# Five stages for split weights, raw transposes in the head, a halved first expert, and w2 stored by output halves

## The chip, the cores and the metric

One NeuronCore of a Trainium2 chip runs the whole kernel. The metric is device time in microseconds of that core: lower is better. A profile of one execution gives the span from its first to its last instruction and what each engine and each DMA queue did in it: PE (matrix products, with PEld for the loading of the stationary operand), DVE (vector), ACT (scalar), POOL, and SP, which here only issues DMAs.

## The reference, cut to what matters

One layer over 256 latent tokens with a context prefix of 256 tokens, D = 1024, all in float32.

```python
mod = silu(c) @ ada_w + ada_b                       # sh1, sc1, g1, sh2, sc2, g2; the same for c_ctx
u  = modulate(rmsnorm(x,   norm1_g), sh1,  sc1)     # modulate(u, shift, scale) = u * (1 + scale) + shift
uc = modulate(rmsnorm(ctx, norm1_g), sh1c, sc1c)
y  = token_mixer(u, uc, ...)                        # u @ w_in, mLSTM (4 heads), differential attention
                                                    # (8 heads), w_branch_a, w_branch_b, gates, w_out
x  = x + g1 * y
x  = x + g2 * moe_ffn(modulate(rmsnorm(x, norm2_g), sh2, sc2))
return rmsnorm(x, final_norm_g)

# moe_ffn: the 4 best of 32 experts for each token; an expert is
hcat  = xf[tok] @ w1[e] + b1[e]                     # w1[e]: 1024 x 2048
h_glu = min(hcat[:, :D_FF], 7);  h_lin = clip(hcat[:, D_FF:], -7, 7)
act   = h_glu * sigmoid(1.702 * h_glu) * (h_lin + 1)
out   = act @ w2[e] + b2[e]                         # w2[e]: 1024 x 1024
```

## The kernel before, in words

The order of the work is written out by hand: each engine takes its instructions in the order in which the program emits them, and semaphores between engines follow from who reads and writes which tile. A tile of a pool with a fixed number of buffers can be written again only when everything that reads its predecessor is done.

**Head.** x and ctx are loaded (L205, L207), their squares summed (L234, L236), and 1/rms made with nine small DVE operations and four diagonal blocks `dg` (L240). `xpose(k)` (L281) multiplies a block of x or ctx by `dg`, which turns and scales it in one product. `ada_first(j)` (L262) makes the shift and scale of 256 channels out of two 1 MB pieces of `ada_w1`, ACT copies the sum (L265), PE turns it (L266) and DVE makes A1 and B1 (L270 to L272). `u_first` (L287 on DVE, L290 on ACT) applies them, `u_second` splits the result in `uh` (ACT cast, L293) and `ul` (DVE, L294). Four rounds j = 0..3 of two channel blocks each are interleaved with the first steps of the first projection chunk.

**Projections.** A `Chunk` is 512 columns of a weight matrix in eight steps of 128 rows. `split(k)` turns raw weights into a rounded part `wh` (ACT, L567) and a remainder `wl` (DVE, L568), in the pool `stg` with 3 buffers of each; `step(k)` multiplies (three products for each result block: L581 to L583 or L591 to L593). A full chunk has 12 products of 512 columns in a step, a half chunk the same count of 256 columns, or six of 512. The main loop emits `split` for up to LOOK = 2 steps ahead, then `step`, then a few ticks of side work: the second part of the modulation (`ada_rest`, L309 and L311, which reads `ada_w2`), the gates, the mLSTM units (L395 to L441), the attention units (L483 to L515) and what follows the chunks. Raw weights, `ada_w1` and `ada_w2` go through a ring of R1 = 4 pieces of 1 MB; a piece is loaded by SP (L159) when its slot is free. At the end come w_branch_b (its evacuation L765, then `late_b`: L771 on DVE, L772 on ACT, L773 on DVE), and w_out, whose second half is first scaled on DVE (`scaled_columns`, L842).

**Experts.** The pools of the projections are closed and their memory becomes places for expert weights (`PLACES`, `ORDER`, `AGAIN`; `slot`, `epiece`, L1014 and L1018): four 2 MB pieces of w1 and two of w2 per expert, 12.6 MB, 32 experts. SP issues a piece when its place is free. `hidden` multiplies (L1070), applies the activation (L1081 to L1085), turns the result (L1090, copied by ACT at L1091); `expert` multiplies with w2 (L1104); `scatter` adds to the sums `xs` (L1125, L1118). Experts 30 and 31 are taken together at the end: `out_half(dh, fh)` loads 512 of the 1024 columns of half a w2 (L1256) and multiplies (L1259), `half_gated` (L1263) and `half_back` (L1269) follow, then the last norm (L1217 to L1225) and the output (L1229 to L1233).

Of the kernel before, what the change touches and what calls it, by code (L numbers as in the profile page):

```python
# [10 lines left out]
F32 = mybir.dt.float32  # L11
# [18 lines left out]
R1, LOOK, LATE = 4, 2, 6  # L30
# [3 lines left out]
HOMES = dict(xc=[0], wk=[1, 2], mk=[3], mv=[4, 5], sums=[6, 7], hm=[8], dk=[1, 3], dv=[2, 4], og=[0], ah=[6], al=[7],  # L34
# [76 lines left out]
def hybrid_layer(ctx: ExitStack, tc, a, out, dbg=None):  # L111
# [40 lines left out]
    fr = ExitStack()  # L152
    ring = fr.enter_context(tc.tile_pool(name="ring", bufs=R1))
# [37 lines left out]
    xs = keep.tile([128, 2, D], F32, name="xs")  # L191
# [38 lines left out]
    xm = [xc[:, 0], xc[:, 1], x1[:, 0], x1[:, 1]]  # L230
    for m in (2, 3, 0, 1):
# [15 lines left out]
    quarters = [(j, h) for j in range(4) for h in range(2)]
    aw = {}

    def ada_load(n):  # L250
        for _ in range(n):
            if quarters:
                j, h = quarters.pop(0)
                aw[j, h] = piece(a["ada_w1"][j, h], 8, 256)

    def ada_first(j):
        q = slice(128 * j, 128 * j + 128)
        for h in range(2):
            for kk in range(4):
                k = 4 * h + kk  # L260
                for g in range(4):
                    mm(S0[32 * g:32 * g + 32, 0, q], sil[:, k, :], aw[j, h][:, 2 * kk + g // 2, 128 * (g % 2):128 * (g % 2) + 128],  # L262
                       start=(k == 0), stop=(k == KT - 1))
        mod = t2([128, 128], "mod0")
        act.copy(mod, S0[:, 0, q])  # L265
        tr(S0[:, 1, q], mod, ident)  # L266
        pv = S0[:, 1, q].rearrange("p (g b s) -> p s g b", g=2, b=2)
        c = slice(2 * j, 2 * j + 2)
        over = lambda v: v[:, None, c].to_broadcast([128, 2, 2])
        dve.tensor_tensor(out=A1[:, :, c], in0=pv[:, 0:2, 1], in1=over(abT[:, 1]), op=OP.add)  # L270
        dve.tensor_tensor(out=B1[:, :, c], in0=pv[:, 0:2, 0], in1=over(abT[:, 0]), op=OP.add)
        dve.tensor_tensor(out=A1[:, :, c], in0=A1[:, :, c], in1=over(ng1), op=OP.mult)  # L272
# [3 lines left out]
    us, xt = {}, {}  # L276

    def xpose(k):
        xt[k] = pp()
        for m in range(4):  # L280
            mm(xt[k][:, m * 128:(m + 1) * 128], xm[m][:, k * 128:(k + 1) * 128], dg[m], start=True, stop=True)  # L281

    def u_first(k):
        us[k] = t2([128, 512], "u")
        for m, s in ((0, slice(256, 512)), (1, slice(0, 256))):
# [1104 lines left out]
```

## Time and profile before

| | us |
|---|---|
| median of 3 runs (lowest, highest) | 1423.0 (1422.38, 1424.02) |
| the profiled execution's own time | 1420.2 |
| its span, first to last instruction | 1418.5 |
| PE busy / DVE busy / ACT busy | 1331.5 / 556.2 / 288.5 |
| DMA read from HBM | 480 MB, 339 GB/s over the span |

The span has three parts: head and projections up to about 488 us, 30 experts in pairs up to about 1310 us, the last two experts and the norm. Busy shares over the whole span say little, since each part has another limit; the rows further down are from views that keep the parts asunder: the span in slices, the chain of waits in order of time, busy time by stretch, single instructions in order of time, and who waited for whom.

### The profile page before, as it was taken

The numbers are of one execution on the slowest core, as the hardware profiler recorded it, in microseconds if no ns is written. First come the engines' busy times: TensorE is split into PE (matmuls) and PEld (weight loads), VectorE is DVE, ScalarE is ACT, GpSimd is POOL, SyncE is SP. The second block draws the span as 40 slices with busy tenths as digits, with TensorE's granted clock in tenths as the row PEclk, the third lists the DMA queues.
The fourth block names the chain that finished last, engine by engine and source line by source line (L and its number), as shares of the span: only waits on it lengthen the run. The fifth ranks groups of instructions, "written<-read, shape, count | busy, mean of one in ns | idle before, by whom it ended". The sixth has DMA issues, their size and how long they took to land.

```text
span 1418.5 us, 17043 instructions
## 1 busy us (share of the span) xinstructions
PE 1331.5 (94%) x6981; PEld 713.5 (50%) x6981; DVE 556.2 (39%) x1181; ACT 288.5 (20%) x620; POOL 36.2 (3%) x55
## 2 busy tenths in 40 slices
PE   5999999999998999999999999999999999999996
PEld 4778777778988734434434433333332333323332
DVE  3586765686667612222222323222212322123113
ACT  3434334444553311101101101011000100001001
POOL 0030001000010000000000000000000000000000
PEclk9999999999999999999999999999999999999999
DMA  9666343223358799999999999999999999999995
GB/s 361 216 250 231 120 156 119 90 90 113 126 190 360 315 369 410 432 429 430 432 428 431 432 429 431 430 430 432 430 431 431 430 429 433 429 430 432 429 416 198
DMA packets 45070, 482.30 MB, mean 340 GB/s; under 512 B 5619, under 2 KB 5876, under 8 KB 11580
## 3 DMA queue, kind: packets, MB, share of 16 engines
q1 hardware_dynamic: 44268, 479.82, 81.9%
q8 instruction: 57, 0.93, 0.2%
q0 software_dynamic: 432, 0.81, 0.2%
q10 hardware_dynamic: 288, 0.52, 0.1%
q14 instruction: 25, 0.20, 0.0%
HBM read 480.08 MB, written 1.06 MB: 339 GB/s over the span
## 4 chain that ended last, share of the span: by engine, by line
PE 58%; DMA 31%; DVE 6%; ACT 2%; issue 1%; SPq 1%; ACTq 0%; DVEq 0%
PE acc L1070 15%; PE py L1104 9%; PE acc L591 4%; PE acc L593 4%; PE acc L592 3%; PE pga L1036 3%; PE acc L581 3%; PE acc L582 3%; DMA v__6686<-in_w_dram 3%; PE acc L583 3%; DMA v__7709<-in_w_dram 3%; DMA v__7935<-in_w_dram 3%; DMA vA__8179<-in_w_dram 3%; DMA v__6212<-in_w_dram 3%; DMA vA__7138<-in_w_dram 3%; DMA v__7364<-in_w_dram 3%
## 5 line engine op out<-in xcount | busy, mean ns | idle before, releaser
L1081 DVE TENSOR_SCALAR eg<-acc 128x512 f32<-128x512 f32 (+1 forms) x33 | 22.3, 675 | 417.1 <-PE acc L1070 417.1
L1082 ACT ACTIVATE es<-eg 128x512 f32<-128x512 f32 (+1 forms) x33 | 20.4, 617 | 687.8 <-DVE eg L1081 687.8
L568 DVE TENSOR_TENSOR wl<-w,wh 128x512 fp32r<-128x512 f32 (+1 forms) x160 | 106.8, 674 | 85.0 <-ACT wh L567 84.2
L1112 DVE TENSOR_TENSOR Y<-py,g2r 64x512 f32<-64x512 f32 x60 | 41.3, 689 | 239.4 <-PE py L1104 238.7
L591 PE MATMUL acc<-uh,wh 128*128 128x256 f32 (+1 forms) x328 | 109.0, 332 | 0.7 <-ACT wh L567 0.7
L567 ACT CAST wh<-w 128x512 fp32r<-128x512 f32 (+1 forms) x160 | 93.1, 603 | 60.9 <-PE acc L583 28.5
L593 PE MATMUL acc<-uh,wl 128*128 128x256 f32 (+1 forms) x328 | 104.3, 318 | 0.3 <-DVE wl L568 0.2
L592 PE MATMUL acc<-ul,wh 128*128 128x256 f32 (+1 forms) x328 | 104.1, 317 | 0.0
L591 PEld LDWEIGHTS acc<-uh,wh 128*128 128x128 f32 x328 | 61.9, 189 | 12.9 <-ACT wh L567 3.9
L581 PE MATMUL acc<-wh,uh 128*128 128x512 f32 x160 | 65.9, 412 | 0.7 <-DVE gi L348 0.7
L593 PEld LDWEIGHTS acc<-uh,wl 128*128 128x128 f32 x328 | 61.7, 188 | 5.6 <-DVE wl L568 0.7
L592 PEld LDWEIGHTS acc<-ul,wh 128*128 128x128 f32 x328 | 61.9, 189 | 4.4 <-DVE ul L294 0.3
L582 PE MATMUL acc<-wl,uh 128*128 128x512 f32 x160 | 63.6, 398 | 0.0
L583 PE MATMUL acc<-wh,ul 128*128 128x512 f32 x160 | 63.5, 397 | 0.0
L815 PE MATMUL acc<-b1s,cst 128*64 128x512 f32 x256 | 61.7, 604 | 0.0
L1036 PE MATMUL pga<-P,x 128*128 128x128 f32 x512 | 60.1, 275 | 0.4 <-DVE P L938 0.4
L1036 PEld LDWEIGHTS pga<-P,x 128*128 128x128 f32 x512 | 58.5, 192 | 0.6 <-DVE P L938 0.5
L1125 PE MATMUL acc<-Y,PGT 128*128 128x512 f32 x120 | 55.8, 606 | 0.0
L311 DVE SCALAR_TENSOR_TENSOR sums<-w,sil,sums 128x512 f32<-128x512 f32 x56 | 42.5, 774 | 0.0
L1118 DVE TENSOR_TENSOR xs<-xs,acc 128x512 f32<-128x512 f32 x60 | 37.4, 679 | 7.0 <-PE acc L1269 7.0
L1070 PE MATMUL acc<-ws,XG 128*64 128x512 f32 x176 | 39.7, 593 | 0.0
L1125 PEld LDWEIGHTS acc<-Y,PGT 128*128 128x128 f32 x120 | 21.5, 189 | 34.0 <-issue 20.8
(680 smaller groups left out, 2088.2 us busy)
## 6 DMA issues: line engine op xcount, KB each, us to landing
ws<-in_w_dram SPq DMA_DIRECT2D x20, 2048.0 KB, 35.2
w<-in_w_in_dram SPq DMA_DIRECT2D x30, 1024.0 KB, 4.8
w<-in_ada_w_dram SPq DMA_DIRECT2D x24, 1024.0 KB, 5.9
w<-in_w_a_dram SPq DMA_DIRECT2D x4, 1024.0 KB, 4.9
wo<-in_w_o_dram SPq DMA_DIRECT2D x4, 1024.0 KB, 4.9
w<-in_w_b_dram SPq DMA_DIRECT2D x4, 1024.0 KB, 9.2
ws<-in_w_dram SPq DMA_DIRECT2D x3, 1024.0 KB, 13.4
wk<-in_w_in_dram SPq DMA_DIRECT2D x2, 1024.0 KB, 13.4
```

The lines of the kernel that those rows point to most:

```text
L567: act.copy(wh[:, 0:n], raw)
L568: dve.tensor_tensor(out=wl[:, 0:n], in0=raw, in1=lanes(wh[:, 0:n]), op=OP.subtract)
L581: mm(self.ps[j], vh[:, k, s], wh, start=st, stop=False)
L582: mm(self.ps[j], vh[:, k, s], wl, start=False, stop=False)
L583: mm(self.ps[j], vl[:, k, s], wh, start=False, stop=sp)
L591: mm(o, wh[:, c], vh[:, k, t0:t1], start=f, stop=False, skip_group_check=g)
L592: mm(o, wh[:, c], vl[:, k, t0:t1], start=False, stop=False, skip_group_check=g)
L593: mm(o, wl[:, c], vh[:, k, t0:t1], start=False, stop=sp, skip_group_check=g)
L1036: mm(p[:, kk, 0:n * CAP], x1[:, tt, k * 128:k * 128 + 128], P[:, tt].rearrange("p e s -> p (e s)"), start=(tt == 0), stop=(tt == 1))
L1070: mm(G[f // 2][64 * (f % 2):64 * (f % 2) + 64], XG[:, k, sw * CAP:sw * CAP + CAP], w[:, f * 512:f * 512 + 512], start=False, stop=(k == KT ...
L1104: mm(Y[r:r + 64], aT_[:, j, fh * 64:fh * 64 + 64], w[:, dh * 512:dh * 512 + 512], start=(kf == 0), stop=(kf == KT - 1))
L1125: mm(p, PGT[parts[dh], 2 * dh + tt, :], Y2[parts[dh], dh], start=True, stop=True)
```

## The change

1. **Stages.** LOOK goes from 2 to 4. A second pool `stg2` with 2 buffers of `wh` and `wl` is added; of five splits in a row three go to `stg`, two to `stg2`. `stg2` takes 8 KB of each partition; the sums `xs` (8 KB) leave the pool `keep` and get a pool of their own after the projections' pools are closed, where `stg2` lay.
2. **Head.** x and ctx are turned raw, before 1/rms is known (`turn`, plain transposes), and copied to two tiles `raw` in the buffers that `mv` uses later. 1/rms is spread over rows by four products (`scale_rows`). `u_of` multiplies raw by it, then applies A1 and B1 for one block. `ada_w1` is stored so that one 1 MB piece serves one block of 128 channels; `ada_first(j)` is for one block, and one product with `fold` (64 columns) adds and turns it. The pieces are loaded in another order: the first ahead of the first projection weights, three more before the second half of these, four as slots come free.
3. **First expert.** Its activation goes in two halves of 256 columns (`parts=2`); the turned gates of the first pair use PSUM bank `py`, not `ptr`; a Sigmoid of one element is issued before the expert loop.
4. **w2.** It is stored with the 512 columns of an output half together. In an expert, both output halves read from the two halves of a piece; in `out_half` a load has 8 KB (the last ones 4 KB) in a row for each partition, where it had rows of 2 KB.
5. **End.** `half_gated` and `half_back` of the last quarter go in two parts of 256 columns; the first output DMA goes through SP, not ACT.

```diff
-R1, LOOK, LATE = 4, 2, 6
+R1, LOOK, LATE = 4, 4, 6
+HOMES: raw=[4, 5]                                  # mv=[4, 5] as before
+    stg2 = fr.enter_context(tc.tile_pool(name="stg2", bufs=2))
-    xs = keep.tile([128, 2, D], F32, name="xs")
+    xs = tp("xs", 1).tile([128, 2, D], F32, name="xs")      # after fr.close()
...
+    def ada_load():
+        if eighths:
+            j = eighths.pop(0)
+            aw[j] = piece(a["ada_w1"][j], 8, 256)
     load_small("ng1T", "ada_bT")
+    ada_load()
...
+    def turn(m):
+        for hf in range(2):
+            p = acc()
+            for k in range(4):
+                tr(p[:, k * 128:k * 128 + 128], xm[m][:, (4 * hf + k) * 128:(4 * hf + k) * 128 + 128], ident)
+            dst, src = raw[hf][:, :, m * 128:m * 128 + 128], p.rearrange("p (k t) -> p k t", k=4)
+            (dve.tensor_copy if hf else act.copy)(dst, src)
     for m in (2, 3, 0, 1):                         # squares as before
+            if m == 3:
+                turn(2)
+                turn(3)
     rs1 = rstd_of(...); dg = ...                   # as before
+    turn(0)
+    turn(1)
...
     def ada_first(j):
+        q = slice(128 * (j % 4), 128 * (j % 4) + 128)
+        for k in range(KT):
+            for b in range(2):
+                g = 2 * (k % 2) + b
+                mm(S0[32 * g:32 * g + 32, 0, q], sil[:, k, :], aw[j][:, k, 128 * b:128 * b + 128],
+                   start=(k < 2), stop=(k >= KT - 2))
+        mods[j] = t2([128, 128], "mod0")
+        act.copy(mods[j], S0[:, 0, q])
+    def ada_turn(j):
+        pt = pp()
+        mm(pt[:, 0:64], mods.pop(j), fold, start=True, stop=True)
+        dve.tensor_scalar(A1[:, :, j], ...); dve.tensor_scalar(B1[:, :, j], ...)
+    def scale_rows():
+        for m in range(4):
+            mm(rsr[0][:, m * 128:m * 128 + 128], ones, dg[m], start=True, stop=True)
+    def u_of(k):
+        dve.tensor_tensor(out=u, in0=raw[k // 4][:, k % 4], in1=rsr[0], op=OP.mult)
+        # then A1, B1 in two halves (k even: DVE, odd: ACT), act.copy to uh, dve subtract to ul
...
     def split(self, k):
-            wh = stg.tile([128, 512], F32R, name="wh")
-            wl = stg.tile([128, 512], F32R, name="wl")
+            at = stg if nsplit[0] % 5 < 3 else stg2
+            nsplit[0] += 1
+            wh = at.tile([128, 512], F32R, name="wh")
+            wl = at.tile([128, 512], F32R, name="wl")
...
     first.load(0)
+    for _ in range(3):
+        ada_load()
     first.load(1)
+    ada_first(0)
+    scale_rows()
+    ada_turn(0)
+    first.split(0)
+    ada_first(1)
+    u_of(0)
+    first.split(1)
+    ada_load()
+    ada_turn(1)
+    for k in range(KT):
+        if k + 2 < KT:
+            ada_first(k + 2)
+        if k + 1 < KT:
+            u_of(k + 1)
+        ada_load()
+        if k + 2 < KT:
+            first.split(k + 2)
+            first.step(k)
+            ada_turn(k + 2)
...
-                mm(Y[r:r + 64], aT_[:, j, fh * 64:fh * 64 + 64], w[:, dh * 512:dh * 512 + 512],
+                mm(Y[r:r + 64], aT_[:, j, fh * 64:fh * 64 + 64], w[dh][:, j * 512:j * 512 + 512],
+    warm = mt.tile([1, 1], F32, name="warm")
+    act.activation(warm, ones[0:1, 0:1], AF.Sigmoid)
-                        nxt["PGT0"] = transposed(PG, 2)
+                        nxt["PGT0"] = transposed(PG, 2, "py")
-            Y = expert(..., gates_turned if (pr, sw) == (LATE, 1) else None)
+            Y = expert(..., gates_turned if (pr, sw) == (LATE, 1) else None, 1 if e else 2)
-            nc.scalar.dma_start(rows_of[:, 0:512], xo[:, tt, 0])
+            (nc.scalar if tt else nc.sync).dma_start(rows_of[:, 0:512], xo[:, tt, 0])
...
     def out_half(dh, fh):
-        step = 2 if dh and fh else 4
-        for k0 in range(0, 4, step):
+        step = 1024 if dh and fh else 2048
+        for k0 in range(0, 2048, step):
             for i in range(2):
-                src = a["w2"][E - 2 + i, fh].rearrange("p (k n) -> p k n", k=4)
-                nc.sync.dma_start(w[i][:, k0:k0 + step], src[:, k0:k0 + step, s])
+                nc.sync.dma_start(w[i][:, k0:k0 + step], a["w2"][E - 2 + i, fh][:, 2048 * dh + k0:2048 * dh + k0 + step])
-    half_gated(1)
-    half_back(1)
+    half_gated(1, 2)
+    half_back(1, 2)
...
-    r["ada_w1"] = f(ada[:, 0:2 * D].reshape(2, 4, 128, 2, 4, 256).transpose(4, 0, 2, 1, 3, 5)).reshape(4, 2, 128, 2048)
+    r["ada_w1"] = f(ada[:, 0:2 * D].reshape(KT, 128, 2, KT, 128).transpose(3, 1, 0, 2, 4)).reshape(KT, 128, 2048)
-    r["w2"] = rows(f(i["exp_w2"]).reshape(E * D, D), 4).reshape(E, 2, 128, 4 * D)
+    r["w2"] = f(f(i["exp_w2"]).reshape(E, 2, 4, 128, 2, 512).transpose(0, 1, 3, 4, 2, 5)).reshape(E, 2, 128, 4 * D)
```

## Rows read from the trace of the kernel before

**Rows 1.** Page, 40 equal slices: DMA rate.

```profile
GB/s 361 216 250 231 120 156 119 90 90 113 126 190 360 315 369 410 432 429 430 432 428 431 432 429 431 430 430 432 430 431 431 430 429 433 429 430 432 429 416 198
```

**Rows 2.** Chain that ended last, in order of time: start us, us, what.

```profile
768.74 33.80 DMA v__5982<-in_w_dram
...
901.65 3.46 PE py L1104 x16
```

**Rows 3.** Busy time of each engine by stretch, PE clock, DMA share, GB/s.

```profile
492.70:510.00 17.30, 16.97 (x94) 8.16 (x96) 4.40 (x24) 2.04 (x6) 0.31 (x1) 1.00 0.94 347
769.00:1330.00 561.00, 526.66 (x2496) 199.40 (x2494) 138.33 (x278) 41.42 (x84) 2.96 (x10) 1.00 1.01 430
1372.00:1400.00 28.00, 25.81 (x111) 8.95 (x108) 5.10 (x11) 1.50 (x4) 0.00 (x0) 1.00 0.94 363
```

**Rows 4.** SP's DMA issues in order of time: start us, us, what.

```profile
520.42 0.33 SPq L1018 DMA_DIRECT2D v__4961<-in_w_dram  x1
...
547.49 0.33 SPq L1018 DMA_DIRECT2D ws<-in_w_dram  x1
```

**Rows 5.** Head, chain in order of time: PE's turning and modulation products.

```profile
13.39 3.74 PE pp L281 x16
...
31.62 1.78 PE pp L281 x16
36.21 1.93 PE S L262 x64
```

**Rows 6.** Head, single instructions: loads that land, and POOL.

```profile
9.67 1.06 ACT L234 ACTIVATE junk<-xc 128x1024 f32<-128x1024 f32 x1 [1.38 <-DMA xc<-in_ctx_dram]
17.07 1.15 ACT L567 CAST wh<-wk 128x512 fp32r<-128x512 f32 x2 [6.24 <-DMA wk<-in_w_in_dram]
43.27 0.77 POOL L146 DMA_DIRECT2D lamr<-in_lam_dram  x1 [0.96 <-PE pp L281]
```

**Rows 7.** First products of the first chunk's steps 6 and 7.

```profile
51.47 0.39 PE L591 MATMUL acc<-uh,wh 128*128 128x512 f32 x1
...
54.34 0.40 PE L591 MATMUL acc<-uh,wh 128*128 128x512 f32 x1
```

**Rows 8.** PE's waits up to 490 us: total us, times, longest us.

```profile
PE pp L429 <- ACT hm L437: 5.4, 4, 2.8
PE acc L591 <- ACT wh L567: 2.2, 3, 0.9
PE acc L581 <- ACT wh L567: 1.7, 1, 1.7
PE acc L593 <- DVE wl L568: 1.4, 4, 0.6
```

**Rows 9.** End of the projections: a single instruction, and the stretch with PE's clock.

```profile
459.45 0.69 DVE L773 TENSOR_TENSOR yl<-tg,yh 128x512 fp32r<-128x512 f32 x1 [0.68 <-ACT yh L772]
455.00:475.00 20.00, 17.93 (x70) 13.27 (x70) 15.43 (x26) 8.73 (x17) 0.00 (x0) 0.91 0.99 407
```

**Rows 10.** First expert, between its two products.

```profile
510.93 1.28 ACT L1082 ACT_TABLE_LOAD   x1 [12.30 <-DVE eg L1081]
513.73 0.63 PE L1090 MATMUL ptr<-cst,el 128*128 128x128 f32 x4 [2.17 <-DVE el L1085]
515.03 5.35 PE L1104 MATMUL py<-v__4796,eaT 128*64 128x512 f32 x16 [0.67 <-ACT eaT L1091]
```

**Rows 11.** Last expert (two halves) and end: waits and issues.

```profile
1382.66 0.42 DVE L1081 TENSOR_SCALAR eg<-acc 128x256 f32<-128x256 f32 x1 [14.37 <-PE acc L1070]
1387.07 0.64 PE L1259 MATMUL pga<-v__8287,eaT 128*64 128x512 f32 x1
1396.07 0.64 PE L1259 MATMUL pga<-ws,v__8216 128*64 128x512 f32 x1 [1.06 <-DMA ws<-in_w_dram]
1412.54 0.72 ACT L1229 ACTIVATE v__8130<-v__8130,rsfy 128x512 f32<-128x512 f32 x1 [0.49 <-ACT v__8130 L1229]
```

**Rows 12.** Page, DMA issues: what, times, KB each, median us to landing.

```profile
w<-in_w_in_dram SPq DMA_DIRECT2D x30, 1024.0 KB, 4.8
```

More of the change, by code (lines that the diff above doesn't have):

```diff
@@ L213, in load_small @@
             nc.sync.dma_start(small[n], a[n])
+    eighths = list(range(KT))
+    aw = {}
+    def ada_load():
+        if eighths:
+            j = eighths.pop(0)
+            aw[j] = piece(a["ada_w1"][j], 8, 256)
     load_small("ng1T", "ada_bT")
+    ada_load()
     sil = sm.tile([128, KT, 32], F32, name="sil")
@@ L230, in hybrid_layer @@
     xm = [xc[:, 0], xc[:, 1], x1[:, 0], x1[:, 1]]
+    raw = [b8([128, 4, 512], "raw") for _ in range(2)]
+    def turn(m):
[5 more added lines that the diff above has]
+            (dve.tensor_copy if hf else act.copy)(dst, src)
     for m in (2, 3, 0, 1):
@@ L244, in hybrid_layer @@
     B1 = sm.tile([128, 2, KT], F32, name="B1")
+    fold = early.tile([128, 64], F32, name="fold", tag="eb")
     ng1, abT = small["ng1T"], small["ada_bT"]
     pool.tensor_scalar(abT[:, 1], abT[:, 1], 1.0, None, op0=OP.add)
[L247 to L254, printed above, removed]
-    def ada_first(j):
[L257 to L272, printed above, removed]
@@ new lines, in hybrid_layer @@
+    pool.tensor_tensor(out=fold, in0=ident[:, 0:64], in1=ident[:, 64:128], op=OP.add)
+    mods = {}
+    def ada_first(j):
+        q = slice(128 * (j % 4), 128 * (j % 4) + 128)
[6 more added lines that the diff above has]
+        act.copy(mods[j], S0[:, 0, q])
@@ L278, in xpose @@
-    def xpose(k):
-        xt[k] = pp()
+    rsr = []
+    def scale_rows():
+        rsr.append(pp())
         for m in range(4):
[L281 to L285, printed above, removed]
+            mm(rsr[0][:, m * 128:m * 128 + 128], ones, dg[m], start=True, stop=True)
+    def u_of(k):
+        u = t2([128, 512], "u")
+        dve.tensor_tensor(out=u, in0=raw[k // 4][:, k % 4], in1=rsr[0], op=OP.mult)
+        for m, c in ((0, slice(256, 512)), (1, slice(0, 256))):
@@ L286, in u_first @@
             if k % 2 == 0:
-                dve.tensor_scalar(us[k][:, s], xt[k][:, s], A1[:, m, k:k + 1], B1[:, m, k:k + 1],
-                                  op0=OP.mult, op1=OP.add)
-            else:
-                act.activation(us[k][:, s], xt[k][:, s], AF.Identity, scale=A1[:, m, k:k + 1], bias=B1[:, m, k:k + 1])
-    def u_second(k):
-        act.copy(uh[:, k], us[k])
-        dve.tensor_tensor(out=ul[:, k], in0=us[k], in1=lanes(uh[:, k]), op=OP.subtract)
+                dve.tensor_scalar(u[:, c], u[:, c], A1[:, m, k:k + 1], B1[:, m, k:k + 1], op0=OP.mult, op1=OP.add)
+            else:
+                act.activation(u[:, c], u[:, c], AF.Identity, scale=A1[:, m, k:k + 1], bias=B1[:, m, k:k + 1])
@@ L297, in hybrid_layer @@
+        act.copy(uh[:, k], u)
+        dve.tensor_tensor(out=ul[:, k], in0=u, in1=lanes(uh[:, k]), op=OP.subtract)
     work = Work()
@@ L533, in hybrid_layer @@
     w_in = a["w_in"]
+    nsplit = [0]
     class Chunk:
@@ L886, in hybrid_layer @@
     first = chunks[0]
-    ada_load(2)
     first.load(0)
-    ada_load(2)
+    for _ in range(3):
+        ada_load()
     first.load(1)
-    for j in range(4):
-        ks = (2 * j, 2 * j + 1)
-        for k in ks:
-            xpose(k)
-        if j:
-            first.step(2 * j - 2)
-        for k in ks:
-            first.split(k)
-        ada_first(j)
-        ada_load(2)
-        for k in ks:
-            u_first(k)
-        for k in ks:
-            u_second(k)
-        if j:
-            first.step(2 * j - 1)
+    ada_first(0)
[17 more added lines that the diff above has]
+            ada_turn(k + 2)
     ahead = KT
@@ L1051, in gated, with transposed @@
         return PG
-    def transposed(PG, n):
+    def transposed(PG, n, bank="ptr"):
         PGT = mt.tile([128, 4, 128], F32, name="PGT", tag="PGT", bufs=2)
-        p4 = bank1("ptr")
+        p4 = bank1(bank)
         for i in range(4):
@@ L1093, in hidden, with expert @@
         return aT_
-    def expert(XG, sw, G, w1p, w2p, between, after=lambda: None, mid=None):
-        aT_ = hidden(XG, sw, G, w1p, between, after, mid=mid)
+    def expert(XG, sw, G, w1p, w2p, between, after=lambda: None, mid=None, parts=1):
+        aT_ = hidden(XG, sw, G, w1p, between, after, mid=mid, parts=parts)
         Y = bank1("py")
@@ L1198, in after @@
                     G01[e + 1] = bias_of(e + 1)
-            Y = expert(XG, sw, G01.pop(e), w1_of(e), w2p, between, after, gates_turned if (pr, sw) == (LATE, 1) else None)
+            Y = expert(XG, sw, G01.pop(e), w1_of(e), w2p, between, after, gates_turned if (pr, sw) == (LATE, 1) else None, 1 if e else 2)
             evac_y(Y2, Y, sw)
```

35 lines of the change are left out of this document (21 added, 14 removed).

## The prediction

> **What bounds the kernel now.** I read the slices first [rows 1]. From the 17th slice (567 us) to the 38th the DMA rate stands at 428 to 433 GB/s: a ceiling, 430 GB/s over 561 us of the expert part [rows 3]. Before that it is mostly far lower: the projections leave the DMA idle half the time. The chain of waits in order of time then says when this ceiling begins to hold PE: at 768.74 us PE waits for an expert piece for the first time, 33.80 us [rows 2], and from there pieces are the chain until close to the end. So the kernel is a head and projections set by PE (with DVE), a start of the expert part in which PE frees places and the DMA follows, then a stretch that runs at the DMA's own pace, then a short tail.
>
> Three consequences, on which the sum rests. First, work that PE saves between 570 and 1310 us is worth nothing. Second, what shifts the moment at which the DMA stream becomes unbroken shifts the end by as much, since the bytes behind it are the same. Third, that moment is not 488 us. Between 492.7 and 510 us the stream moved 347 GB/s, not 430 [rows 3]; and SP issued pieces at 520.42 and 547.49 us [rows 4] when PE had just freed their places and the stream had run dry or nearly so. So the first expert's PE time, up to about 547 us, still counts in full; so does every microsecond of the projections, whose end frees the places.
>
> **Head.** In before PE does nothing until 13.39 us: it waits for `dg`. Then each pair of channel blocks costs one turning group (1.78 us, the first at the lower clock 3.74 us), one modulation group (1.93 us) [rows 5] and two steps of 54.34 - 51.47 = 2.87 us [rows 7]. The last step began at 54.34, so the first chunk ended at 57.2 us. The change takes the four turning groups off: 3.74 + 3 x 1.78 = 9.1 us. In their place stand 32 transposes. Four of them took 0.63 us [rows 10], so eight groups are 5 us at most, twice that at the lower clock; those of ctx can run from 9.67 us [rows 6] and those of x a megabyte's time sooner, while PE has nothing else to do. Their copies (four each on ACT and DVE, by the 0.6 to 0.7 us of a 512-column operation, as L773 at 0.69 us [rows 9]) lie in the same empty time, beside the 1/rms chain. New on the path: four products for `scale_rows` (half a turning group, 0.9 us, before the first ada piece is used up) and one small `fold` product per block, about 0.2 us (bounds 0.1, and 0.3 as a transposing product with its wait). Where does it start? ctx landed at 9.67, the third megabyte behind it at 17.07 us [rows 6], 2.5 us each. The new order is ada 0, wk 0, ada 1, ada 2, so ada 2 is there at 19.6 us; its group of half size (0.97 us) stands ahead of step 0 on PE, which so begins at about 20.8. From there PE is the bound: 8 x 2.87 + 5 x 0.97 + 6 x 0.2 = 29.0 us, and about 1 us in which step 7 waits for its block (fold, A1, multiply, ACT twice, cast, subtract in a row). End at 50.8 us against 57.2: **6.4 us**. DVE gets a multiplication more per block (0.69 us, bounds 0.5 to 0.8), some 2.8 us per round of 4.0, so it stays covered; without that cover a round would cost the excess. Later ada loads, one per round of 4 us against 2.5 us per megabyte, are covered by PE's rounds.
>
> POOL: `raw` lies in the buffers of `mv`, so the two `mv` memsets, early in POOL's queue, now wait for the last reading of `raw`, about 45 us. Behind them stand the broadcast of lambda (before at 43.27 us [rows 6]), the router's constants and two norm scales. Only lambda is wanted soon, by DVE at the end of the first chunk: 0 to 1 us of DVE time, I take 0, as DVE has idle time there.
>
> **The clock.** The first 16 turning products took 3.74 us against 1.78 later [rows 5]: PE did these at 1.2 GHz and the rest at 2.4 GHz. In the new head PE works from 7 us on, with holes between 14 and 19.6 us while it waits for loads. If the rise comes only while step 0 runs, the ada group and the fold ahead of it and some 2.1 us of its work take twice as long: 0.97 + 0.2 + 2.1 = 3.3 us lost. I take no loss, since by then PE has done more than what stood ahead of the rise in before; it is a rival below. The Trainium skill, "TensorE: Matmul & The Clock Gate", Part 4: PE-mode transpose, speaks against that: transposes do not count as PE activity for the clock. By that rule the early transposes would buy no clock, and the head would give 3.1 us instead of 6.4. No row here shows transposes alone ahead of a rise, so the trace does not decide it.
>
> **Stages.** The stage that split i+4 writes is freed by step i-1, just as split i+2 with three stages: ACT and DVE reach no further back in PE's work than before, and the mLSTM's waits (5.4 us for `hm` [rows 8]) stay. What changes is that PE holds two more finished splits. PE's waits for `wh` and `wl` are 2.2 + 1.7 + 1.4 = 5.3 us [rows 8]; most lie at the ends of w_branch_b and the start of w_out, and with them PE's clock fell: 0.91 over 20 us [rows 9], 1.8 us of cycles. Together 7.1 us. Not all comes back. Around w_branch_b's second halves DVE has more to do than PE: per step of a half chunk (half of 2.87 us) one split and one scaling (2 x 0.69 [rows 9]), and per chunk an evacuation of two such operations and `late_b` with four, and two waits of 0.68 us for ACT [rows 9]. Two more splits done beforehand are worth 1.4 us; beyond that PE runs into w_out's fifth step, which needs the last `yh`, and I count 2 us of wait there. Another 1.1 us may come back as longer waits for the mLSTM chain. So **4.0 us**, between 1.4 (two splits, nothing else) and 7.1.
>
> Loads: the ring keeps four pieces, and a piece is wanted two steps earlier, but it is also freed two steps earlier. I went through the emission order: from the freeing of a slot to the first split out of it lie 2.5 steps of 2.87 us at the tightest, 7.2 us, against 4.8 us to landing [rows 12]. `xs` is first written in the second pair, long after `stg2` is done: 0.
>
> **First expert.** Between its two products before: a table load of 1.28 us on ACT at 510.93, transposes at 513.73 and the second product at 515.03 us [rows 10]; the activation's first operation, of 0.69 us, ended as the table load began, so 4.8 us lie between. The last expert already does its activation in halves: 1382.66 to 1387.07, 4.4 us [rows 11]. With the table loaded early (ACT is idle there) and the PSUM bank no longer shared, 0.4 us. More hangs on the clock: the 16 products from 515.03 took 5.35 us [rows 10], against 3.46 us for 16 of them later [rows 2], so 1.9 us were lost to the lower level, which came after PE had been idle 2.17 us at one go. In halves the longest hole is some 1.4 us. PE's hole of 1.06 us before 1396.07 [rows 11] was followed by no slow products. So I take **2.3 us**; 0.4 if it falls again. The DMA's holes at 520 us and after can take this up.
>
> **w2 and end.** For experts 0 to 29 a piece is as large as before: 0. In the tail, rows of 2 KB moved 363 GB/s between 1372 and 1400 us [rows 3]: 10.2 MB that would take 23.6 us at 430. Of these 4.4 us PE only waits 1.06 us, at 1396.07 [rows 11]; otherwise it is busy with its own chain. So 1.1 us (0 to 2). The split of the last quarter starts PE 0.27 us sooner, but the first sum is complete only after three of four products: between -0.3 and +0.3, I take 0. ACT's second scaling waited 0.49 us behind its own DMA issue [rows 11]; SP takes that: 0.5 us. **1.6 us**, between 0.2 and 2.8.
>
> **Sum.** 6.4 + 4.0 + 2.3 + 1.6 = 14.3 us, off the profiled execution's 1420.2 us (span 1418.5): 1405.9. The median of the runs is 2.8 us above that execution; off 1423.0 it is **1408.7 us**.
>
> **The rivals.** (a) The clock rises late in the head: 3.3 us less, 1412.0. For it: holes of PE up to 19.6 us. Against it: the transposes and two ada groups that PE has done by then. (b) DVE's pace holds the end of the projections, so the stages give 1.4 us only: 1411.3. (c) The gains do not arrive, as the stream binds already before 500 us: only the tail is left, 1421.4. Against it: 347 GB/s [rows 3] and issues that follow PE [rows 4]. (d) Slower: the ring of raw weights. With splits two steps further ahead, ACT, which takes its work in order, stands in front of a piece that has not landed, and behind it stand the evacuations and gates; 16 ada pieces compete for the same four slots until 160 us. It decides where less than 4.8 us [rows 12] lie between freeing and need. PE has four steps, 11.5 us, in hand, so each miss must be repeated to reach PE; six misses at 4.8 us would be 29 us: 1438. (e) The first expert's clock falls again: 1410.6.
>
> **How the numbers follow.** The forecast, with (e) and smaller misses of its terms: 0.57. (a) 0.20, (b) 0.11, (c) 0.05, (d) 0.07. All terms at their upper bounds give 1423.0 - (7.0 + 7.1 + 2.3 + 2.8) = 1403.8; (a) and (b) together with 0.4 for the first expert and 0.6 for the tail give 1423.0 - (3.1 + 1.4 + 0.4 + 0.6) = 1417.5. The range is 1403.5 to 1417, which leaves out (c), (d) and a little of the rest. 0.2% (2.8 us) is about what a measurement of this kernel can tell from no change: faster 0.88, same 0.05, slower 0.07.
>
> **What would show it.** The copy of the first chunk's result on ACT about 6.4 us earlier; no PE wait for `wh` or `wl` above 1 us and PE's clock near 1.00 in the 20 us at w_out; the first expert's second product 4.4 us after its activation began, 16 of them in 3.5 us; no DMA wait at the third quarter of the tail. SP's pieces of the first two experts should be issued 11 to 13 us earlier, and the first long wait of PE for an expert piece should come that much earlier as well. I am wrong if these shifts are there and the end is not shifted alike, or if ACT waits for raw weights again and again between 50 and 160 us.

## The result, and the profile after

The changed kernel takes **1408.8 us** (median of 6 runs, 1406.3 to 1412.4), the kernel before 1423.5 (6 runs, 1422.4 to 1424.9): a ratio of 0.9901, 95% interval 0.9885 to 0.9917. The forecast was 1408.7. The changed kernel's profiled execution took 1408.9 us (span 1407.2), that of before 1420.2 (1418.5). So the two profiles lie 11.3 us apart and the medians 14.7: the forecast's 14.3 us are in the medians, but not in the two traces that it was made for. That gap is the main question below.

First, the answers to the rows of before. PE in the head (start us, us, engine line op, out<-in, shape, count, [idle before, and what ended it]); L246 are the new transposes, L289 the `fold` products, L613 the first step:

```profile
7.29 3.65 PE L246 MATMUL acc<-cst,x 128*128 128x128 f32 x16 [7.29 <-DMA x<-in_x_dram]
10.72 2.01 PE L246 MATMUL acc<-cst,xc 128*128 128x128 f32 x16
...
16.09 0.33 PE L289 MATMUL pp<-fold,mod 128*128 128x64 f32 x2
...
20.59 0.49 PE L613 MATMUL acc<-uh,wh 128*128 128x512 f32 x1
```

Against [rows 5] the turning groups are gone, and step 0 begins at 20.59 us (20.8 was worked out). PE had done nothing but transposes when the second 16 of them ran in 2.01 instead of 3.65 us: the clock had come up. (This is read from the durations: the profile's column of the granted clock stands at 1.00 from the start, over the slow 16 as well.) ACT's copy of the first chunk's result begins at 49.35 us; before, at 55.24:

```profile
49.35 0.59 ACT L660 COPY mk<-acc 128x512 f32<-128x512 f32 x1 [0.75 <-PE acc L615]
```

```profile
55.24 1.29 ACT L638 COPY mk<-acc 128x512 f32<-128x512 f32 x2 [0.63 <-PE acc L593]
```

That is 5.9 us, of which 1.2 are lost at once, when PE waits for the gates; behind them PE's waits at w_out:

```profile
62.20 0.47 PE L603 MATMUL acc<-wh,uh 128*128 128x512 f32 x1 [1.83 <-DVE gi L366]
...
452.72 0.50 PE L603 MATMUL acc<-wh,yh 128*128 128x512 f32 x1 [1.77 <-ACT wh L589]
453.52 0.50 PE L604 MATMUL acc<-wl,yh 128*128 128x512 f32 x1 [0.30 <-DVE wl L590]
455.90 0.80 PE L603 MATMUL acc<-wh,yh 128*128 128x512 f32 x1 [0.80 <-ACT wh L589]
```

Of the waits in [rows 8], those for `wh` and `wl` are gone up to 445 us, but not the one at the start of w_out. The stretches of the changed kernel (from:to us, length, busy time of PE, PEld, DVE, ACT, POOL, PE's granted clock, DMA share, GB/s):

```profile
440.00:480.00 40.00, 36.78 (x186) 29.21 (x184) 26.22 (x49) 15.82 (x31) 0.00 (x0) 0.91 0.77 296
456.00:462.00 6.00, 5.99 (x15) 4.36 (x16) 3.75 (x7) 2.81 (x6) 0.00 (x0) 0.54 0.86 311
...
769.00:1330.00 561.00, 527.14 (x2514) 202.29 (x2512) 142.51 (x286) 43.30 (x89) 2.96 (x10) 1.00 1.01 430
```

The clock still falls behind these waits: 0.91 over 40 us is 3.6 us of cycles, against 0.91 over 20 us, 1.8 us, in [rows 9]. The ceiling of 430 GB/s is that of [rows 3]. The first expert, against [rows 10]:

```profile
504.46 0.44 PE L1117 MATMUL ptr<-cst,el 128*128 128x128 f32 x2 [0.93 <-DVE el L1112]
506.21 0.66 PE L1117 MATMUL ptr<-cst,el 128*128 128x128 f32 x2 [1.31 <-DVE el L1112]
506.80 4.86 PE L1131 MATMUL py<-v__4860,eaT 128*64 128x512 f32 x16
```

The holes are smaller (0.93 and 1.31 us instead of 2.17 and 0.67), yet the 16 products took 4.86 us, and the granted clock from 500 to 510 us is 0.83: it fell here too. SP issues the pieces of [rows 4] 8.7 us earlier (11 to 13 were forecast):

```profile
511.70 0.33 SPq L1045 DMA_DIRECT2D v__5025<-in_w_dram  x1
...
538.76 0.33 SPq L1045 DMA_DIRECT2D ws<-in_w_dram  x1
```

PE's first long wait for an expert piece comes at 813.61 us, later than in [rows 2] and not earlier, as I had written; but the kernel before, run once more, has it at 825.28, so this mark tells nothing of the change. In the tail the wait for the third quarter (1.06 us in [rows 11]) is 0.4:

```profile
813.61 36.95 DMA v__6276<-in_w_dram
```

```profile
PE pga L1286 <- DMA ws<-in_w_dram: 0.4, 1, 0.4
```

### The profile page after: what moved, and what is told of

The parts are those of the page before. It is cut to its first block, busy times and chain, and to the rows that moved or that the text cites. A ratio compares the mean times of both kernels' runs of the same rounds, so it can differ in the third digit from the quotient of the medians.

```text
span 1407.2 us, 17083 instructions
## 1 busy us (share of the span) xinstructions
PE 1329.6 (94%) x6973; PEld 713.1 (51%) x6973; DVE 564.2 (40%) x1202; ACT 291.2 (21%) x631; POOL 37.0 (3%) x56
## 3 DMA queue, kind: packets, MB, share of 16 engines
HBM read 480.08 MB, written 1.06 MB: 342 GB/s over the span
## 4 chain that ended last, share of the span: by engine, by line
PE 60%; DMA 32%; DVE 5%; ACT 1%; issue 1%; SPq 0%; ACTq 0%; DVEq 0%
PE acc L1097 15%; PE py L1131 9%; PE acc L613 4%; PE acc L614 4%; PE acc L615 4%; PE pga L1063 3%; PE acc L603 3%; PE acc L604 3%; PE acc L605 3%; DMA v__6750<-in_w_dram 3%; DMA v__7773<-in_w_dram 3%; DMA v__8172<-in_w_dram 3%; DMA v__8301<-in_w_dram 3%; DMA v__6976<-in_w_dram 3%; DMA vA__7202<-in_w_dram 3%; DMA v__7428<-in_w_dram 3%
## 5 line engine op out<-in xcount | busy, mean ns | idle before, releaser
L613 PE MATMUL acc<-uh,wh 128*128 128x256 f32 (+1 forms) x328 | 109.1, 333 | 0.3 <-DVE dv L730 0.2
L613 PEld LDWEIGHTS acc<-uh,wh 128*128 128x128 f32 x328 | 61.7, 188 | 14.0 <-issue 4.1
L1152 PEld LDWEIGHTS acc<-Y,PGT 128*128 128x128 f32 x120 | 21.5, 189 | 34.0 <-issue 20.8
## 6 DMA issues: line engine op xcount, KB each, us to landing
w<-in_w_b_dram SPq DMA_DIRECT2D x4, 1024.0 KB, 10.9
```

The lines of the kernel that those rows point to most:

```text
L613: mm(o, wh[:, c], vh[:, k, t0:t1], start=f, stop=False, skip_group_check=g)
L1152: mm(p, PGT[parts[dh], 2 * dh + tt, :], Y2[parts[dh], dh], start=True, stop=True)
```

## The experiments

Every trace was laid against the first trace of before: for each PE product that both kernels have, its start there minus its start here, so that a positive number is a lead. Below it stands at seven times (us of before), then for the moment at which 320 MB of the stream are left (655 us before), and for the end (difference of spans). Differences in the text are taken before rounding.

| lead, us, at | 56 | 70 | 330 | 445 | 485 | 530 | 320 MB left | end | median of runs |
|---|---|---|---|---|---|---|---|---|---|
| changed kernel | 5.9 | 4.7 | 6.3 | 7.3 | 8.0 | 8.7 | 9.3 | 11.3 | 1408.8 |
| e1 stages alone | -2.7 | -3.8 | -2.3 | -1.2 | -0.5 | -1.8 | -1.2 | -2.2 | 1420.1 |
| e2 head alone | 5.8 | 5.8 | 6.0 | 5.9 | 5.8 | 2.8 | 3.3 | 3.1 | 1415.4 |
| e3 first expert alone | -1.9 | -1.9 | -2.4 | -2.7 | -2.6 | -1.9 | -1.3 | -1.9 | 1422.1 |
| e4 w2 and end alone | -0.1 | -0.1 | 0.2 | 0.1 | -1.7 | -2.9 | -2.3 | -1.2 | 1421.8 |
| before once more | -0.1 | -0.1 | 0.3 | 0.2 | -1.7 | -2.9 | -2.2 | -2.3 | 1422.0 |
| e9 before + transposes | 0.8 | 0.8 | 0.4 | 0.0 | 0.1 | -1.2 | -0.8 | -1.2 | 1422.6 |
| e5 eight fillers | 6.2 | 3.5 | 4.8 | 4.1 | 6.9 | 4.3 | 5.1 | 5.8 | 1415.2 |
| e6 scaling on POOL | 6.1 | 3.4 | 4.7 | -4.2 | 2.4 | 1.4 | 2.2 | 3.8 | 1414.6 |
| e7 late look | 6.1 | 6.1 | 8.0 | 9.1 | 10.1 | 12.2 | 12.8 | 14.1 | 1407.7 |
| e10 e7 + results scaled | 3.9 | 3.9 | 3.6 | 3.1 | 8.8 | 10.5 | 10.7 | 11.1 | 1406.8 |
| e11 two fillers | 6.2 | 5.0 | 8.1 | 7.5 | 10.4 | 12.6 | 13.5 | 14.6 | 1407.2 |
| e12 e10 + e11 | 5.8 | 5.8 | 8.2 | 9.3 | 15.0 | 15.1 | 15.6 | 16.2 | 1406.6 |

Beside these runs the kernel before had medians of 1421.7 to 1422.5. What was expected of e1 to e4 weighs two accounts: the forecast's terms (6.4, 4.0, 2.3, 1.6), and the trace of the changed kernel taken at its word (head 5.9, stages 2, first expert 0.7, w2 and end 2).

**e1: the stages alone**

```diff
-R1, LOOK, LATE = 4, 2, 6
+R1, LOOK, LATE = 4, 4, 6
+    stg2 = fr.enter_context(tc.tile_pool(name="stg2", bufs=2))
...
+            at = stg if nsplit[0] % 5 < 3 else stg2
```

> Only the five stages and the splits four ahead, on the kernel before. The forecast's terms: 4.0 us faster than before, PE's waits for wh and wl gone, none added. What the trace of the changed kernel suggests: the splits now stand ahead of the copies of the gates on DVE, so PE's wait for gi (L348 in before, 0.8 us) grows by about 1.1 us near 60 us, then 1.5 us come back near 300 us and 1.7 at the end of the projections: 1.9 us faster in all. If DVE's pace held the end of the projections alone and nothing were lost at the gates, 1.4 us.

2.4 us faster by the ratio (0.9983, interval 0.9971 to 0.9995). Within the trace the head, which is that of before, lost 2.7 us to the clock (below). From 56 us on, -1.2 at the gates, +1.5 by 330 us, +1.1 by 445 and +0.7 at w_out: 2.2 us, as in the changed kernel (5.9 to 8.0). PE's wait at the gates (total, times, longest), first here, then in e2, where splits go two ahead:

```profile
PE acc L585 <- DVE gi L348: 1.9, 1, 1.9
```

```profile
PE acc L599 <- DVE gi L366: 0.7, 1, 0.7
```

**e2: the head alone**

```diff
+    def turn(m):
...
+    def scale_rows():
...
-            xpose(k)
+    scale_rows()
```

> Only the new head, with two splits ahead as before. The forecast: the copy of the first chunk's result (mk) and the end 6.4 us earlier. The trace of the changed kernel suggests 5.9 us at mk, and, if the 0.9 us that it lost again at the gates belong to the splits issued further ahead and not to the head, 5.9 us also at 120 us and at the end; if they belong to the head (the later broadcast of lambda, or the clock), about 5.0 us from 60 us on. If the clock rose only with step 0, 3.1 us.

0.9949 (0.9935 to 0.9963): 7.3 us. In the trace 5.8 us at the end of the head, kept up to 485 us (behind that this execution loses 3 us in the gather and the first expert, with the clock at 0.89 and 0.83 there); so what the changed kernel loses at the gates belongs to the stages, and the later broadcast of lambda costs nothing. The 7.3 us of the medians (5.3 to 9.2) contain the trace's 5.8. If they are really more, a cause is at hand, though not shown: the old head's clock does not always come up once and stay. Over 14 to 30 us it was 1.00 in the first profile of before, but 0.89 in e1 (below) and in e3, which have the same head and lost 2.7 and 1.9 us there.

```profile
14.00:30.00 16.00, 13.97 (x152) 12.25 (x154) 5.14 (x11) 4.56 (x9) 0.00 (x0) 0.89 0.92 387
```

**e3: the first expert alone**

```diff
-                        nxt["PGT0"] = transposed(PG, 2)
+                        nxt["PGT0"] = transposed(PG, 2, "py")
...
+    act.activation(warm, ones[0:1, 0:1], AF.Sigmoid)
...
-            Y = expert(XG, sw, ...)
+            Y = expert(XG, sw, ..., 1 if e else 2)
```

> Only the first expert's part: activation in halves, the transposes of the gate in another bank, the table loaded early. The forecast: 2.3 us faster, the clock staying up. The trace of the changed kernel suggests 0.7 us, the second product's 16 instructions at 4.9 us or more, as the clock falls there again. If the DMA's holes at 520 us swallow it: 0.

0.9995 (0.9985 to 1.0005), not to be told from nothing. In the trace 0.7 us (-2.6 to -1.9), with a second product at the lower clock, as the second account has it:

```profile
516.83 0.66 PE L1090 MATMUL ptr<-cst,el 128*128 128x128 f32 x2 [1.25 <-DVE el L1085]
517.41 4.89 PE L1104 MATMUL py<-v__4804,eaT 128*64 128x512 f32 x16
```

**e4: w2's layout and the end alone**

```diff
-                nc.sync.dma_start(w[i][:, k0:k0 + step], src[:, k0:k0 + step, s])
+                nc.sync.dma_start(w[i][:, k0:k0 + step], a["w2"][E - 2 + i, fh][:, 2048 * dh + k0:2048 * dh + k0 + step])
...
+    half_gated(1, 2)
+    half_back(1, 2)
```

> Only the layout of w2 and the end. The forecast: 1.6 us faster (1.1 from rows of 8 KB in the tail, 0.5 from the output's DMA on another queue). The trace of the changed kernel suggests 2.0 us, as its shift grew by that much behind 1366 us. If the tail had been hidden behind PE: 0.5.

0.9999 (0.9990 to 1.0009): not to be told from nothing. In the trace the lead grows by 1.1 us from the stream to the end. The stretch for which before has 363 GB/s [rows 3] runs at 392:

```profile
1372.00:1400.00 28.00, 26.54 (x118) 8.85 (x114) 5.10 (x11) 1.50 (x4) 0.00 (x0) 1.00 0.94 392
```

Over all traces this growth is 0.4 to 2.0 us (mean 1.1) for the eight kernels with the new end, and -1.0 to -0.1 (mean -0.4) in e1, e2, e3, e9 and before once more: about 1.5 us. By their ratios the four parts alone give 2.4 + 7.3 + 0.7 + 0.1 = 10.5 us. The four intervals, each 1.3 to 2.0 us to a side, are too wide to say whether the rest of the 14.7 lies between the parts.

**before once more**, unchanged.

> The kernel before, unchanged, once more. In four executions of its unchanged head the clock came up once and stayed (0 and 0.1 us against the profiled execution of before) or fell again for a moment (1.9 and 2.7 us lost). If that spread is what puts its median 2.3 to 3.3 us above its first profiled execution, this profile either ends near 1420 with a head at 0, or near 1422 with 1.9 to 2.7 us lost before 30 us.

Neither of the two: it took 1422.5 us with its head at -0.1. It lost 1.8 us at w_out and 1.3 in the first expert, at waits that the first profile has too. Granted clock over the two stretches, in this execution and then in the first profile (whose 455 to 475 us stand in [rows 9], 0.91):

```profile
455.00:475.00 20.00, 17.68 (x62) 12.83 (x61) 13.62 (x23) 7.25 (x13) 0.00 (x0) 0.83 0.99 412
510.00:525.00 15.00, 12.16 (x48) 4.01 (x46) 4.55 (x12) 2.97 (x4) 0.29 (x1) 0.77 0.88 363
```

```profile
510.00:525.00 15.00, 12.16 (x54) 4.16 (x52) 5.68 (x14) 2.97 (x4) 0.29 (x1) 0.89 0.96 388
```

So the execution on which the forecast rests was one in which the clock fell for little. What the same wait costs differs from one execution to the next: over those 20 us the clock was 0.91 in before, 0.83 in its repetition and in e4, and 1.00 in e3 and e9, all with the same code there.

**e9: before, with transposes ahead of everything**

```diff
+            for q in ((2, 3) if m == 3 else (0, 1)):
+                for hf in range(2):
+                    p = acc()
+                    for k in range(4):
+                        tr(p[:, k * 128:k * 128 + 128], xm[q][...], ident)
```

> The kernel before with 32 transposes added ahead of its first product, of ctx and x, whose results nobody reads; nothing is removed. If transposes alone raise the clock, as the changed kernel's trace suggests: the clock rises near 11 us, the first turning group takes 1.8 us instead of 3.74, the wobble that cost 1.9 and 2.7 us in the heads of two other executions of the unchanged head is gone, and the run is 2 to 4 us faster than before. If they do not count for the clock: it rises near 17 us as before and the time is that of before, or up to 0.5 us longer.

```profile
7.32 3.65 PE L241 MATMUL acc<-cst,x 128*128 128x128 f32 x16 [7.32 <-DMA x<-in_x_dram]
10.76 2.48 PE L241 MATMUL acc<-cst,xc 128*128 128x128 f32 x16
13.48 0.71 PE L286 MATMUL pp<-dg,xc 128*128 128x128 f32 x4 [0.24 <-DVE dg L245]
...
18.54 0.33 PE L271 MATMUL S<-cst,mod 128*128 128x128 f32 x1 [1.13 <-ACT mod L270]
```

The clock came up on transposes alone, and the first turning group took 2.0 us (13.48 to 15.46) instead of 3.74 [rows 5]. But PE's wait for ACT's copy of the modulation sum grew (1.13 us; 0.39 in before): 0.8 us are left in the head, and the runs show nothing (1.0004, 0.9993 to 1.0015). The expected 2 to 4 us were wrong: here ACT's copies take up what an early clock gives, as long as the turning products stay.

**e7: the late look**

```diff
-        while ahead <= min(i + LOOK, len(steps) - 1):
+        look = LOOK if i >= 2 * KT else 2
+        while ahead <= min(i + look, len(steps) - 1):
```

> The changed kernel, but splits are issued two ahead until the gates' chunk is done and four ahead only from there. If the splits that stand ahead of the gates' copies on DVE are what cost 1.16 us near 60 us: PE's wait for gi is 0.8 us again and the shift of 5.9 us against before holds at 70 us, 1.1 us faster than the changed kernel. If the wait has another cause (lambda's broadcast, which now lands later): it stays.

1407.7 us (0.9900, 0.9883 to 0.9917). The wait for `gi` is 0.67 us, the lead at 70 us 6.1 instead of 4.7: the splits in front of the gates' copies on DVE were the cause. In e5 and e6, which have the changed kernel's code there, the clock fell behind this wait as well (0.83 from 60 to 70 us; 1.00 in the changed kernel), and they lose 2.7 us between 56 and 70 us instead of 1.2. In this execution the clock did not fall in the first expert, though the holes are the same 0.93 and 1.31 us, and it gave 2.1 us there (10.1 to 12.2):

```profile
60.88 0.47 PE L603 MATMUL acc<-wh,uh 128*128 128x512 f32 x1 [0.67 <-DVE gi L366]
...
504.14 0.41 PE L1118 MATMUL ptr<-cst,el 128*128 128x128 f32 x2 [1.31 <-DVE el L1113]
504.48 3.65 PE L1132 MATMUL py<-v__4860,eaT 128*64 128x512 f32 x16
```

Against the changed kernel the runs do not tell 1.1 us.

**e5 and e11: products that nobody uses, in the holes of the first expert** (eight in e5; one in each hole in e11)

```diff
+        pf = bank1("pga", 2) if parts == 2 and sw == 0 else None
...
+            if pf is not None:
+                mm(pf[0:64], XG[:, 0, 0:CAP], x1[:, 0, 0:512], start=True, stop=True)
```

> The changed kernel with eight products that nobody uses in the two holes of PE in the first expert's activation (three of 0.22 us, then five). If PE's idling there is what lowers the clock: no fall near 506 us, the second product's first 16 in 3.5 us instead of 4.9, 1.4 to 1.7 us faster than the changed kernel (1407.2). If the clock falls for what PE did earlier: no gain, 1408.8.

> The changed kernel with one unused product in each hole of PE in the first expert's activation; such a product took 0.93 us in the run with eight of them, which was too many, and the holes are 0.93 and 1.31 us. If idle PE there lowers the clock: no fall between 500 and 515 us, the second product's first 16 in 3.65 us instead of 4.86, 1.2 to 1.5 us faster than the changed kernel. If whether the clock falls there is set by what lies before (it did not fall in the late look, which has the same holes): no difference that the runs can tell.

e5 first, then e11:

```profile
504.55 2.79 PE L1119 MATMUL pga<-x,XG 128*64 128x512 f32 x6
507.27 0.44 PE L1122 MATMUL ptr<-cst,el 128*128 128x128 f32 x2
507.64 4.50 PE L1119 MATMUL pga<-x,XG 128*64 128x512 f32 x10
...
512.44 3.65 PE L1136 MATMUL py<-v__4869,eaT 128*64 128x512 f32 x16
```

```profile
501.06 1.07 PE L1117 MATMUL pga<-x,XG 128*64 128x512 f32 x2
...
502.44 1.07 PE L1117 MATMUL pga<-x,XG 128*64 128x512 f32 x2
503.81 0.41 PE L1120 MATMUL ptr<-cst,el 128*128 128x128 f32 x2 [0.30 <-DVE el L1112]
504.15 3.65 PE L1134 MATMUL py<-v__4863,eaT 128*64 128x512 f32 x16
```

In e5 a product took 0.9 us, not 0.22 (section on the hardware), so PE came 4 us late to its transposes: 1415.2 us, a miss of my sizing. In e11 they fit. The clock stayed up in both, and e11 gains 2.1 us in the first expert (10.4 to 12.6), but so do e7 and e10 without fillers (2.1 us each, from 495 us on). With the halved activation and no fillers the clock fell there in three executions (the changed kernel, e3, e6) and not in two (e7, e10); with fillers it fell in none of three (e5, e11, e12). Whether filling does anything is **not settled**; e11's 1407.2 us (1405.6 to 1412.8) are not to be told from the changed kernel's.

**e6: the scaling of w_out's second half on POOL**

```diff
-            dve.tensor_tensor(out=v[:, k], in0=v[:, k], in1=rows_[0][:, 512:1024], op=OP.mult)
+            pool.tensor_tensor(out=v[:, k], in0=v[:, k], in1=rows_[0][:, 512:1024], op=OP.mult)
```

> The changed kernel with the eight scalings of w_out's second half (L864, 5.5 us of DVE) on POOL, which is idle there. If DVE's pace sets the end of the projections: PE's waits for wh and wl near 453 us and the fall of the clock behind them are gone, 3 to 5 us faster than the changed kernel. If the chain behind the last yh (ACT and DVE waiting for each other) sets it: at most 1 us. If POOL at some 2 us each is late with its weights: slower.

1414.6 us, slower than the changed kernel, and for none of the three reasons. POOL's eight operations ran from 426.47 us, and DVE's small ones beside them took 1.2 us each, about a POOL operation's 9.88 / 8. First POOL and DVE here, then DVE in the changed kernel, which does the same operations without POOL:

```profile
426.47 9.88 POOL L864 TENSOR_TENSOR wo<-wo,rows 128x512 f32<-128x512 f32 x8 [10.03 <-PE acc L615]
```

```profile
426.29 0.16 DVE L141 TENSOR_SCALAR rso1v<-sso 128x8 f32<-128x8 f32 x1
426.49 1.30 DVE L127 TENSOR_SCALAR rso1y<-rso1v 128x8 int32<-128x8 int32 x1
427.83 1.19 DVE L129 TENSOR_TENSOR rso1t<-rso1y 128x8 f32<-128x8 f32 x1
```

```profile
423.40 0.17 DVE L127 TENSOR_SCALAR rso1y<-rso1v 128x8 int32<-128x8 int32 x1
423.61 0.17 DVE L129 TENSOR_TENSOR rso1t<-rso1y 128x8 f32<-128x8 f32 x1
```

Eight such steps are a chain at whose end PE waits 6.8 us for `od` (lead 4.1 to -4.2). The Trainium skill, "GPSIMD Engine Reference", section 1. Specifications, has POOL's SBUF interfaces shared with VectorE, with contention for DVE instructions with two SBUF inputs or in a 2-port mode; the 0.17 against 1.2 us of L129 agree with that. L127 with its one input took 1.30 us, and no run shows which mode it ran in. The question of DVE's pace stayed open: the wait of 1.77 us at w_out is gone here too, but PE came there late.

**e10: the results scaled instead of the weights** (on e7)

```diff
-            for i in range(2):
-                yield from scaled_columns(chunks[-1].ws[i])
...
+                    dve.tensor_tensor(out=ps[j], in0=ps[j], in1=rows_[0][:, s], op=OP.mult)
                     dve.tensor_tensor(out=x1[:, j, s], in0=x1[:, j, s], in1=ps[j], op=OP.add)
```

> The kernel of the late look (splits four ahead only behind the gates) without the eight scalings of w_out's second half (5.5 us of DVE ahead of w_out); its two results are scaled instead, two DVE operations of 0.69 us behind the last product, as the first half's already are. If DVE's work ahead of w_out holds the end of the projections: PE's waits for wh and wl there (1.75, 0.31 and 0.34 us) and the fall of the clock behind them go, 2 to 4 us in return for 1.4, so 1 to 3 us faster than the late look (1407.7). If the chain behind the last yh sets it: the waits stay, and 1.4 us are added.

Of PE's waits from 440 to 485 us those that bear on this, then the stretch at w_out with PE's clock, here and in e7:

```profile
PE acc L852 <- DVE x L883: 1.6, 2, 0.9
PE acc L603 <- ACT wh L589: 0.3, 1, 0.3
```

```profile
440.00:470.00 30.00, 29.34 (x168) 25.06 (x167) 21.85 (x35) 15.08 (x28) 0.00 (x0) 1.00 0.90 369
```

```profile
440.00:470.00 30.00, 27.46 (x119) 21.17 (x118) 21.28 (x34) 13.53 (x26) 0.00 (x0) 0.89 0.87 359
```

The wait of 1.75 us is gone, the clock does not fall at w_out, and the lead grows from 445 to 485 us by 5.7 us here and in e12, against 0.8 in the changed kernel and 1.0 in e7. The new wait for the scaled results (1.6 us) is in that. So **DVE's work ahead of w_out held the end of the projections**. The run as a whole took 1406.8 us (0.9897, 0.9879 to 0.9914), which the runs do not tell from e7's 1407.7. Its profiled execution is longer than that median (1409.1 us): up to 445 us its lead falls 6.0 us behind e7's. Part of it is lost at waits for DVE near 86 us (1.4 us) and 419 us (1.7 us) that e12, with the same code there, does not have at that length. Its head lost 2.0 us: with the new head the clock fell again in PE's holes there,

```profile
14.00:19.00 5.00, 2.97 (x42) 2.57 (x42) 4.71 (x15) 0.62 (x1) 0.00 (x0) 0.81 1.02 429
19.00:26.00 7.00, 6.62 (x56) 5.05 (x48) 3.50 (x7) 3.70 (x8) 0.00 (x0) 0.65 1.01 422
```

in this one of eight executions with it.

**e12: e7, e10 and the fillers of e11 together**

> The late look, w_out's results scaled instead of its weights, and one unused product in each hole together. If each cause named holds: 1404 to 1406 us, below both kernels. If the DVE operations behind w_out's last product and the products in the holes cost what they bring: 1407 to 1409.

1406.6 us (5 runs, 1403.7 to 1407.3; 0.9891, 0.9874 to 0.9909). In its trace the lead is 16.2 us at the end; on the way it loses 2.1 between 485 and 495 us, with the clock down behind the two waits at L852. Its median is the lowest of all, but its interval overlaps that of the changed kernel.

## Why the prediction came out, point by point

**The time was right, but that it is right to 0.1 us is luck: against the first profile of before, two errors of 3 us cancel.** The terms sum to 14.3 us where the two traces show 11.3, and the 2.8 us by which the median of before lies above its profiled execution did not carry over: the changed kernel's median is that of its profiled execution (1408.8 and 1408.9). The step that failed there is "off 1423.0 it is 1408.7": a difference between an execution and its median was taken for a constant. In before once more it is mostly clock that fell at the wait at w_out and in the hole of the first expert, and the change works on just these.

The table gives a second reading. If the row of before once more is taken off the row of the changed kernel, the parts are 6.0 (head), 3.7 (stages), 2.0 (first expert) and 2.1 us (w2 and end), 13.6 us with the 0.2 lost at the stream: each within 0.6 us of its term. So the terms fit an execution of before in which the clock falls for longer than in the one they were worked out from. How large a part is depends on the execution it is measured against; the points below go by the first profile, the forecast's own.

- **Head, 6.4 us: 5.9.** The order of loads and the start of step 0 were right (0.2 us earlier than worked out). What was mis-sized is the round of step, modulation group and `fold` product: 2.87 + 0.97 + 0.2 = 4.04 us were taken, and from one `fold` to the next it took 4.17 (23.50 to 27.67 us), 4.46 once when PE waited for a piece of `ada_w1`. That makes 0.9 us too many ahead of step 7, against those 0.2 and 0.2 saved at step 7's own wait. Lambda later on POOL cost 0, as taken.
- **Rival (a), a late clock: no.** It rose about when the first 16 transposes were done (10.9 us), on transposes alone; in e9 a little later (the next 16 took 2.48 us, not 2.01), on transposes alone too. The Trainium skill ("TensorE: Matmul & The Clock Gate", Part 4: PE-mode transpose) says that the full clock does not engage for transposes, since they do not count as PE activity in the same way. For the float32 transposes of these two traces that did not hold. (The 3.3 us of this rival held 2.1 us of slow step 0 for which no row was given.) What can happen is another thing: in e10 the clock came up and fell again, which cost 2.0 us.
- **Stages, 4.0 us: 2.1** (1.2 lost, 1.5 + 1.0 + 0.8 gained). Two steps failed. "ACT and DVE reach no further back in PE's work than before" looked only backward: the two further splits stand in front of the gates' copies in DVE's order, and PE waits for those (e1, e2, e7). And at w_out "no PE wait for `wh` or `wl` above 1 us" was forecast, though the term itself counted 2 us of wait there: it was 2.9 us, one of them 1.77, and the clock fell with it. Rival (b) named the cause, DVE's pace, and e10 shows it; only its price was wrong, since the stages still give 2.1 and not 1.4.
- **First expert, 2.3 us: 0.7, or 2.1.** 0.7 where the clock fell (the changed kernel, e3, e6), 2.1 where it did not (e7, e10, e11, e12; e6, e10 and e12 from 495 us on). The term was right for one case, rival (e) for the other. The second product began 4.7 us after the activation (502.13 to 506.80 us), where 4.4 were forecast. "The longest hole is some 1.4 us" was right (1.31), but with that hole the clock falls in some executions and not in others.
- **w2 and end, 1.6 us: 2.0** in the trace, about 1.5 over all traces; e4's own runs (0.1 us, 1.3 to a side) do not show it. The DMA wait at the third quarter is 0.4, not none.
- **Not in the sum:** 0.6 us between PE's lead at 530 us and the stream's (8.7 and 9.3). Before once more has 0.7 of it, so it is the first profile of before, not the change.
- **Rival (c), the stream binds already: no.** No lead at 530 us is more than 0.4 us smaller at the end, and e12's 15.1 us are 16.2 there. **Rival (d), the ring of raw weights: no.** From 40 to 160 us ACT waits for raw weights once, 0.6 us, in the changed kernel and once, 0.5 us, in e1 (2.6 us in before), and e1 is not slower than before.

## What to carry to other kernels

Work issued further ahead on an engine that takes its instructions in order stands in front of everything behind it: look for the small copies that another engine waits for, and let the lead begin after them. When one engine's wait for another survives more buffers, count what the feeding engine does in the steps just before it; here eight scalings of weights against two of results decided it. And before a forecast is set off a median, ask which part of the spread between executions the change touches.

## What the runs showed of the hardware

- The clock rose on transposes alone: 16 in 3.65 us, the next 16 in 2.0 to 2.5 us (the changed kernel and e9).
- The same hole of PE is followed by a fall of the clock in some executions only: the head of before lost 0 to 2.7 us in five executions, and the clock over the 20 us at w_out was 0.83 to 1.00.
- Beside POOL, DVE went at POOL's pace: DVE operations of 0.17 us took 1.2 us, one POOL operation's 1.24 us, while POOL multiplied two operands of 128 x 512 (e6).
- A product of 512 columns that wrote the same 64 rows as the one ahead of it took 0.9 us (e5), while the kernel's, which alternate between two halves of 64 rows, took 0.44 (8 of them, 16 instructions, in 3.5 us). The 0.22 us expected for e5 were 3.5 / 16, an instruction and not a product. Two of the kernel's instructions begin together, as at 511.49 us in the changed kernel; that this is the whole difference was not tried by itself:

```profile
511.49 0.59 PE L1131 MATMUL py<-v__4870,eaT 128*64 128x512 f32 x1
511.49 0.59 PE L1131 MATMUL py<-v__4871,eaT 128*64 128x512 f32 x1
```
